# A hybrid encoder layer on one core: modulation sums on two other engines, and three weight blocks kept one quarter later

## The chip, the cores and the metric

The kernel runs on one core of a Trainium2 chip. The core has a matrix engine (TensorE, PE in the profile), three engines for elementwise work (VectorE as DVE, ScalarE as ACT, GpSimd as POOL), and SyncE (SP), whose queue issues nearly all DMAs here. Each engine executes its own instructions strictly in order and waits on semaphores for the others. The metric is the device time of one execution in microseconds, median of several runs.

## The reference, cut to what matters

One layer: a mixer and a SwiGLU feed-forward block over 2048 positions of 1024 channels, both modulated by six vectors that are computed from one conditioning vector `c`.

```python
c_act = silu(c)
mod = (c_act @ w_ada + b_ada)                  # w_ada is 1024 x 6144
sh1, sc1, g1, sh2, sc2, g2 = split(mod, 6)
h = x * (1.0 + sc1) + sh1
p = h @ w_in                                   # 1024 x 3328, 13 blocks of 256 columns
y = concat(conv_module(...), hgrn2_mixer(...), chunk_attention(...)) @ w_out
x = layer_norm(ALPHA * x + (1.0 + g1) * y)
h = x * (1.0 + sc2) + sh2
gt, up = split(h @ w_ffn_in, 2)
y = (silu(gt) * up) @ w_ffn_out
x = layer_norm(ALPHA * x + (1.0 + g2) * y)
```

## The kernel before

All arithmetic is float32. Each big matmul is done as three passes over operands that are split into a high and a low part: ScalarE casts the high part (`split`, L230), VectorE or GpSimd subtracts it for the low part (L231).

The mixer works through four quarters of 512 positions (`for q in range(NQ)`, L791). A quarter projects the modulated input with the 13 column blocks of `w_in`, runs 62 convolution taps on VectorE (L377), four recurrent heads (`rec_head`), the attention, and the output projection with four blocks of `w_out`. In `rec_head` GpSimd subtracts (L460, and six times L493, tile `tmp<-recB`), ScalarE takes exponentials, VectorE multiplies (L462, L496 to L503), and TensorE multiplies the results (`ktp`, `lp`). The feed-forward part follows from about 1230 us on.

The modulation vector is a sum over the 1024 rows of `w_ada`, each row scaled by an entry of `cact`. The kernel holds 128 rows at a time on the partitions, so a column stretch is a sum of eight scaled tiles (`acc += st * sc`); a matmul with ones then adds over the partitions (`mps`, `rps`).

- `start` (L274) does this for `sh1` and `sc1` (variable `part` 0 and 1) in four steps `kp` of 256 columns. A step loads 8 row tiles of 128x256 for each part (two per DMA, tile `ada_w`), sums them into `tmp`, gets `mod1`, modulates two tiles of the input (`ft`, L239), splits them (`hh`, `hl`), and multiplies them by a quarter of the rows of three weight blocks: the convolution's gate B_AG, its values B_AV, and the first head's B_REC (L308).
- `ada_rest` (L708) is a generator for the other four vectors: eight sums of eight 128x512 tiles (`xb`) into `adac` (L159, L161). The quarter loop advances it by one sum after a head (L810).

Weights: `load_w` (L247) loads a raw quarter block (256 KB), splits it, and stores the split pair (512 KB, `wki<-whl`, L245) to device memory. Later quarters load the stored pair instead of splitting again (`whl<-wki`). Split pairs wait in four buffers (tag `whl`), raw ones in three, the `xb` tiles in four that the output projection uses as well.

The order of each engine's instructions is set by a scheduler that places them by priority and by estimated times; `shifted(tc, -BOOST)` raises a priority. So an edit in one place can move instructions elsewhere.

Of the kernel before, what the change touches and what calls it, by code (L numbers as in the profile page):

```python
# [11 lines left out]
AF = mybir.ActivationFunctionType  # L12
ALU = mybir.AluOpType
# [95 lines left out]
def mixer_phase(tc, es, env):  # L109
    nc = tc.nc  # L110
    NQ = env["NQ"]
    x, xT, bias_d, w_ada, w_in, w_out, rows = (env[k] for k in ("x", "xT", "bias", "w_ada", "w_in", "w_out", "rows"))
    ident, ones, epsc, cact = (env[k] for k in ("ident", "ones", "epsc", "cact"))
# [21 lines left out]
    def tmp(w=Q):  # L135
        return pt.tile([P, 640], F32, name="tmp", tag="tmp", bufs=N_TMP)[:, 0:w]
# [7 lines left out]
    def psum(name):  # L144
        return pm.tile([P, Q], F32, name=name, tag="pm")
# [7 lines left out]
    nc.scalar.activation(out=e0, in_=e0, func=AF.Exp)  # L153
    nc.vector.tensor_tensor(out=cact, in0=c0, in1=e0, op=ALU.mult)

    def add_ada(st, acc, kt, c0):
        nc.sync.dma_start(out=st, in_=w_ada[kt * P:(kt + 1) * P, c0:c0 + 512])
        if kt == 0:
            nc.vector.tensor_scalar(out=acc, in0=st, scalar1=cact[:, 0:1], scalar2=None, op0=ALU.mult)  # L159
        else:  # L160
            nc.vector.scalar_tensor_tensor(out=acc, in0=st, scalar=cact[:, kt:kt + 1], in1=acc,  # L161
                                           op0=ALU.mult, op1=ALU.add)

    def load_ada(alloc, acc, c0):
        for kt in range(KT):
# [2 lines left out]
    def cols_out(acc, ps, dst, one, bc, n=4):  # L168
        for j in range(n):
            nc.tensor.matmul(out=ps[:, j:j + 1], lhsT=acc[:, j * P:(j + 1) * P], rhs=ones[:, 0:1],  # L170
                             start=True, stop=True)
        nc.vector.scalar_tensor_tensor(out=dst, in0=ps[:, 0:n], scalar=one, in1=col(bc, n),
                                       op0=ALU.add, op1=ALU.add)
# [45 lines left out]
    for a in atm:  # L219
# [4 lines left out]
    wkept = {k: tc.dram_tile([4, P, 2, 2, 256], F32R, name=f"wk{k[0]}{k[1]}")  # L224
             for k in [("i", b) for b in range(D_IN // 256)] + [("o", b) for b in range(4)]}
    kept = set()
    state, uhist, kvprev = {}, {}, {}

    def split(src, hi, lo, eng=nc.vector):
        nc.scalar.copy(out=hi, in_=src)  # L230
        eng.tensor_tensor(out=lo, in0=src, in1=hi.bitcast(F32), op=ALU.subtract)  # L231
# [12 lines left out]
    def move(dst, src):  # L244
        nc.sync.dma_start(out=dst.bitcast(F32), in_=src.bitcast(F32))  # L245

    def load_w(key, order, eng=None):  # L247
        parts = {}
        src = (w_in if key[0] == "i" else w_out)[key[1]]
        for kp in order:  # L250
            w = pa.tile([P, 2, 2, 256], F32R, name="whl", tag="whl", bufs=N_W)
            parts[kp] = hi, lo = w[:, 0], w[:, 1]
            if (key, kp) in kept:
                move(w, wkept[key][kp])
                continue
            raw = pa.tile([P, 2, 256], F32, name="wraw", tag="wraw", bufs=N_WRAW)
            nc.sync.dma_start(out=raw, in_=src[:, kp * 2:kp * 2 + 2, :])
            split(raw, hi, lo, eng or (nc.gpsimd if kp % 2 else nc.vector))
            move(wkept[key][kp], w)
            kept.add((key, kp))  # L260
        return parts

    def proj_f(b):
# [10 lines left out]
    def start():  # L274
        nst = 0
        ps = {b: [pool.tile([P, Q], F32, name="pjt", tag=tag) for _ in range(2)]
              for b, pool, tag in ((B_AG, pj, "pj"), (B_AV, pj, "pj"), (B_REC, pm, "pm"))}
        for kp in range(4):
            c0 = kp * 256
            for part in range(2):  # L280
                acc = tmp(256)
                for kk in range(4):
                    i = nst % 22
                    nst += 1
                    if i >= 14:
                        st = pt.tile([P, 2, 256], F32, name="ada_w", tag=f"attk{i % 4}", bufs=2)
                    else:
                        st = pa.tile([P, 2, 256], F32, name="ada_w", tag=f"y{'hl'[i % 2]}{1 + i // 2}")
                    r0 = kk * 256
                    nc.sync.dma_start(out=st, in_=w_ada[r0:r0 + 256, part * D + c0:part * D + c0 + 256].rearrange(  # L290
                        "(k p) c -> p k c", p=P))
                    for k in range(2):
                        sc = cact[:, 2 * kk + k:2 * kk + k + 1]
                        if kk == 0 and k == 0:
                            nc.vector.tensor_scalar(out=acc, in0=st[:, k], scalar1=sc, scalar2=None, op0=ALU.mult)
                        else:
                            nc.vector.scalar_tensor_tensor(out=acc, in0=st[:, k], scalar=sc, in1=acc,
                                                           op0=ALU.mult, op1=ALU.add)
                o = part * 8 + kp * 2
                cols_out(acc, psum("mps"), mod1[:, o:o + 2], float(part),  # L300
                         (C_BSC1 if part else C_BSH1) + kp * 2, 2)
            load_h(0, (2 * kp, 2 * kp + 1))
            for n, b in enumerate(ps):
                w = load_w(("i", b), (kp,), nc.gpsimd if n else nc.vector)[kp]
                for k in range(2):
                    for j in range(2):
                        for n, (a, c) in enumerate(PASSES):
                            nc.tensor.matmul(out=ps[b][j], lhsT=w[a][:, k, j * P:(j + 1) * P],  # L308
                                             rhs=hts[2 * kp + k][c], start=(kp == 0 and k == 0 and n == 0),
                                             stop=(kp == 3 and k == 1 and n == 2))  # L310
        return ps
# [479 lines left out]
    for q in range(NQ):  # L791
        us, k0, V, G = nxt
        if q == 2:
            h2_norm(tc, env, 0)
            h2_norm(tc, env, 1)
        taps = conv_taps(us)
        accs = None
        kbm = k0
        for h in range(4):
            rec_head(q, h, kbm, V, G[h % 2])  # L800
            for _ in range(TAPS[h] if h < 3 else 0):
                accs = next(taps, accs)
            if h == 2:
                conv_back(accs)
            if h < 3:
                kbm = rec_front(h + 1)
            if h == 1:
                V = rec_v(1)
                G = rec_g(1)
            if h < 3 or q == 0:  # L810
                next(rest, None)
            if q >= 2:
                for _ in range(2):
                    next(early, None)
        kvq = att_front(q)
        attention(q, kvq)
        if q + 1 == NQ:
            for _ in rest:
                pass
            as_.close()  # L820
            rs_.close()
            ffn_open(tc, env)
        else:
            nxt = fronts_a(q + 1)
        out_proj(q)
# [389 lines left out]
```

## Time and profile before

| | |
|---|---|
| median of 3 runs | 2593.28 us (2588.7, 2593.28, 2594.78) |
| the profiled execution | 2589.91 us, span of its instructions 2588.2 us |
| TensorE, matmuls | busy 2457.8 us, 95% of the span |
| VectorE | busy 1656.1 us, 64% |
| ScalarE | busy 997.2 us, 39% |
| GpSimd | busy 665.7 us, 26% |
| mean granted TensorE clock | 0.974 |
| DMA | 423.99 MB, mean 164 GB/s |

Busy TensorE time is not the same as full speed: matmuls are pipelined, and at a granted clock of 0.5 the same work takes twice as long. So the share is read stage by stage, and the idle time of TensorE with what ended it counts for more than its sum.

### The profile page before, as it was taken

What the parts mean: (1) busy time and instruction counts of PE and PEld (TensorE: products, weight loads), DVE (VectorE), ACT (ScalarE), POOL (GpSimd) and SP (SyncE); (2) the same over time, 40 slices, a digit from 0 to 9 for tenths busy, and PEclk for the clock granted to TensorE, in tenths of its full rate; (3) what the DMA queues carried; (4) which work ended last, traced back from release to release, by engine and by line L of the source; (5) the groups of instructions that cost most, each with busy time, mean ns of one, the idle gap of its engine ahead of it and who ended that gap; (6) DMA issues with size and microseconds to landing.
All of it is one profiled execution on the core that took longest, in us unless ns stands there. A gap on an engine that the chain in (4) does not pass through costs nothing.

```text
span 2588.2 us, 36360 instructions
## 1 busy us (share of the span) xinstructions
PE 2457.8 (95%) x13274; PEld 2078.5 (80%) x13274; DVE 1656.1 (64%) x2917; ACT 997.2 (39%) x1920; POOL 665.7 (26%) x571
## 2 busy tenths in 40 slices
PE   6888899999999999987999999999999999999998
PEld 5766799879977898876878788888888888888887
DVE  7987696669557785666655555765445474364666
ACT  2444444354244433544323333433333352242333
POOL 3433112200152112510333332332322211111121
PEclk8997999999999999988999999999999999999999
DMA  9676667663755645547333332442222274454544
GB/s 354 212 236 187 186 197 264 201 180 128 241 183 172 205 164 184 191 135 259 102 117 119 118 130 90 164 142 91 74 82 90 74 244 142 130 182 134 161 147 142
DMA packets 202691, 423.99 MB, mean 164 GB/s; under 512 B 20240, under 2 KB 69008, under 8 KB 202512
## 3 DMA queue, kind: packets, MB, share of 16 engines
q1 hardware_dynamic: 202352, 421.15, 49.8%
q8 instruction: 104, 1.70, 0.3%
q14 instruction: 75, 0.61, 0.1%
q0 software_dynamic: 160, 0.52, 0.1%
HBM read 317.78 MB, written 95.42 MB: 160 GB/s over the span
## 4 chain that ended last, share of the span: by engine, by line
PE 78%; DVE 10%; DMA 6%; issue 3%; ACT 2%; POOL 1%; SPq 0%; DVEq 0%; POOLq 0%; ACTq 0%
PE pi L953 31%; PE po L1095 17%; PE pjt L270 11%; PE pjt L321 9%; PE lp L513 2%; DVE cacc L377 2%; PE sc L625 1%; PE tp L661 1%; PE tp L648 1%; DMA whl<-wki 1%; DMA whl<-wko 1%; PE lp L533 1%; DMA xst<-zall 1%; DMA opraw<-srcd 1%; DMA xb<-in_x_dram 1%
## 5 line engine op out<-in xcount | busy, mean ns | idle before, releaser
L953 PE MATMUL pi<-oph,fhi 128*128 128x512 f32 x1232 | 484.1, 393 | 17.8 <-ACT fhi L829 11.9
L953 PE MATMUL pi<-opl,fhi 128*128 128x512 f32 x1232 | 483.7, 393 | 0.0
L953 PE MATMUL pi<-oph,flo 128*128 128x512 f32 x1232 | 478.9, 394 | 0.0
L270 PE MATMUL pjt<-hh,whl 128*128 128x512 f32 x1184 | 402.5, 411 | 16.2 <-DMA whl<-wki 6.4
L953 PEld LDWEIGHTS pi<-oph,fhi 128*128 128x128 f32 x1232 | 232.4, 189 | 70.2 <-ACT fhi L829 12.1
L829 ACT CAST fhi<-fraw 128x512 fp32r<-128x512 f32 x220 | 136.2, 621 | 392.3 <-PE pi L953 376.6
L270 PEld LDWEIGHTS pjt<-hh,whl 128*128 128x128 f32 x1184 | 227.4, 194 | 66.4 <-DMA whl<-wki 6.0
L958 DVE TENSOR_TENSOR fu<-fu,pi 128x512 f32<-128x512 f32 x176 | 120.8, 686 | 245.8 <-PE pi L953 245.1
L953 PEld LDWEIGHTS pi<-opl,fhi 128*128 128x128 f32 x1232 | 232.5, 189 | 52.3
L1095 PE MATMUL po<-oph,alo 128*128 128x512 f32 (+1 forms) x702 | 273.9, 390 | 0.0
L1095 PE MATMUL po<-oph,ahi 128*128 128x512 f32 (+1 forms) x702 | 270.1, 385 | 3.1 <-DVE res L1116 3.1
L1095 PE MATMUL po<-opl,ahi 128*128 128x512 f32 (+1 forms) x702 | 272.6, 388 | 0.0
L953 PEld LDWEIGHTS pi<-oph,flo 128*128 128x128 f32 x1232 | 232.3, 189 | 49.5 <-DVE flo L830 0.2
L830 DVE TENSOR_TENSOR alo<-araw,ahi 128x512 fp32r<-128x512 f32 x172 | 148.5, 871 | 190.9 <-ACT ahi L829 174.3
L270 PE MATMUL pjt<-hl,whl 128*128 128x512 f32 x592 | 243.0, 411 | 0.0
L321 PE MATMUL pjt<-whl,yh 128*128 128x256 f32 x1024 | 196.7, 288 | 15.5 <-DMA whl<-wko 12.0
L830 DVE TENSOR_TENSOR flo<-fraw,fhi 128x512 fp32r<-128x512 f32 x220 | 159.5, 742 | 70.9 <-ACT fhi L829 70.8
L377 DVE SCALAR_TENSOR_TENSOR cacc<-u,cs,cacc 128x512 f32<-128x512 f32 x240 | 195.3, 843 | 0.2
L829 ACT CAST ahi<-araw 128x512 fp32r<-128x512 f32 x172 | 104.9, 618 | 222.3 <-PE po L1095 208.0
L321 PEld LDWEIGHTS pjt<-whl,yh 128*128 128x128 f32 x1024 | 164.1, 194 | 17.7 <-DVE yl L231 7.9
L930 POOL TENSOR_TENSOR ft<-fraw 128x512 f32<-128x512 f32 x43 | 59.9, 1392 | 450.6 <-DMA fraw<-in_w_fi_dram 433.5
L1095 PEld LDWEIGHTS po<-oph,ahi 128*128 128x128 f32 x702 | 132.4, 189 | 31.7 <-DVE res L1116 3.3
(257 smaller groups left out, 4539.1 us busy)
## 6 DMA issues: line engine op xcount, KB each, us to landing
whl<-wki SPq DMA_DIRECT2D x156, 512.0 KB, 3.8
fraw<-in_w_fi_dram SPq DMA_DIRECT2D x86, 512.0 KB, 3.7
araw<-actd SPq DMA_DIRECT2D x154, 256.0 KB, 3.4
wki<-whl SPq DMA_DIRECT2D x52, 512.0 KB, 4.3
whl<-wko SPq DMA_DIRECT2D x48, 512.0 KB, 3.5
actd<-fs SPq DMA_DIRECT2D x44, 512.0 KB, 3.3
xb<-in_w_ada_dram SPq DMA_DIRECT2D x64, 256.0 KB, 4.7
opraw<-srcd SPq DMA_DIRECT2D x56, 256.0 KB, 5.0
```

What stands on the lines that cost most here:

```text
L270: nc.tensor.matmul(out=ps[j], lhsT=w[kt // 2][a][:, kt % 2, j * P:(j + 1) * P], rhs=hts[kt][c], start=(kt == 0 and n == 0), stop=(kt == KT ...
L321: nc.tensor.matmul(out=ps[tt // 2][:, tt % 2, :], lhsT=lhs[2 * kp + k][c][:, tt * P:(tt + 1) * P], rhs=w[kp][a][:, k, :], start=(ko == 0 a ...
L377: nc.vector.scalar_tensor_tensor(out=ac, in0=us[j][:, t:t + Q], scalar=col(wc + t), in1=ac, op0=ALU.mult, op1=ALU.add)
L513: nc.tensor.matmul(out=lp[0:n, c, :], lhsT=ddf[:, c * P:c * P + n], rhs=d4[:, c, :, :], start=True, stop=True)
L533: nc.tensor.matmul(out=lp[:, c, :], lhsT=K[:, 2 * i + c, :], rhs=M[:, 2 * i + c, :], start=True, stop=True)
L625: nc.tensor.matmul(out=sc[:, 0:n + x], lhsT=qs[hd][ph][:, i * P:(i + 1) * P], rhs=kt_[:, o - x0:o - x0 + n + x], start=ph == 0, stop=ph == 1)
L829: nc.scalar.copy(out=hi, in_=src)
L830: nc.vector.tensor_tensor(out=lo, in0=src, in1=hi.bitcast(F32), op=ALU.subtract)
L930: e.tensor_tensor(out=t1, in0=w12, in1=w11, op=ALU.subtract)
L953: nc.tensor.matmul(out=out, lhsT=w[n][a][:, idx, :], rhs=ops[n, idx][c], start=first and idx == 0 and i == 0, stop=idx == NK - 1 and i == ...
L958: nc.vector.tensor_tensor(out=out, in0=a, in1=b, op=ALU.add)
L1095: nc.tensor.matmul(out=pts[j][:, c], lhsT=a[x][:, j * P:(j + 1) * P], rhs=wo[f][y][:, c], start=f == 0 and m == 0, stop=f == NF - 1 and m ...
```

## The change

Three edits.

1. A helper `add_scaled` multiplies a tile by its scalar on ScalarE, in place (into the accumulator for the first tile), and adds it to the accumulator on GpSimd. It is used for the `sc1` half of the sums in `start` and for all sums of `ada_rest`; the `sh1` half stays on VectorE.
2. `start` no longer stores the split pairs of its three blocks (`keep=False`). The second quarter finds nothing kept, loads their raw tiles again, splits them and stores the pairs then; quarters three and four load the pairs as before.
3. `ada_rest` advances after heads 0 to 2 in the first quarter, after all four heads in the second, and after heads 1 and 3 in the third; before, after all four heads in the first quarter and after heads 0 to 2 in each later one.

```diff
+    def add_scaled(acc, st, sc, first):
+        nc.scalar.activation(out=acc if first else st, in_=st, func=AF.Copy, scale=sc)
+        if not first:
+            nc.gpsimd.tensor_tensor(out=acc, in0=acc, in1=st, op=ALU.add)
+
     def add_ada(st, acc, kt, c0):
         nc.sync.dma_start(out=st, in_=w_ada[kt * P:(kt + 1) * P, c0:c0 + 512])
-        if kt == 0:
-            nc.vector.tensor_scalar(out=acc, in0=st, scalar1=cact[:, 0:1], scalar2=None, op0=ALU.mult)
-        else:
-            nc.vector.scalar_tensor_tensor(out=acc, in0=st, scalar=cact[:, kt:kt + 1], in1=acc,
-                                           op0=ALU.mult, op1=ALU.add)
+        add_scaled(acc, st, cact[:, kt:kt + 1], kt == 0)
...
-    def load_w(key, order, eng=None):
+    def load_w(key, order, eng=None, keep=True):
...
-            move(wkept[key][kp], w)
-            kept.add((key, kp))
+            if keep:
+                move(wkept[key][kp], w)
+                kept.add((key, kp))
...
-                        if kk == 0 and k == 0:
+                        first = kk == 0 and k == 0
+                        if part:
+                            add_scaled(acc, st[:, k], sc, first)
+                        elif first:
...
-                w = load_w(("i", b), (kp,), nc.gpsimd if n else nc.vector)[kp]
+                w = load_w(("i", b), (kp,), nc.gpsimd if n else nc.vector, False)[kp]
...
-            if h < 3 or q == 0:
+            if q == 1 or q == 2 and h % 2 or q == 0 and h < 3:
                 next(rest, None)
```

The lines of the changed kernel stand one to five below those of before (L231 becomes L232, L493 becomes L498).

GpSimd's order in `start`, before: the splits of the weights (`whl`) and of the odd input tiles (`hl1`, `hl3`, `hl5`, `hl7`, two digits of the buffer number follow).

```order
L231 TENSOR_TENSOR whl_342<-wraw_343,whl_342 128x512
L231 TENSOR_TENSOR whl_360<-wraw_361,whl_360 128x512
L231 TENSOR_TENSOR hl1_320<-ft_317,hh1_319 128x512
L231 TENSOR_TENSOR hl3_430<-ft_427,hh3_429 128x512
L231 TENSOR_TENSOR whl_452<-wraw_453,whl_452 128x512
L231 TENSOR_TENSOR whl_470<-wraw_471,whl_470 128x512
L231 TENSOR_TENSOR hl5_540<-ft_537,hh5_539 128x512
```

The same place in the changed kernel, from the second weight split to `hl1`; `tmp_289`, `tmp_403` and `tmp_517` are the `sc1` sums of steps 0, 1 and 2 (of the 15 adds between, the last ten are shown).

```order
L159 TENSOR_TENSOR tmp_403<-tmp_403,ada_w_409 128x256
L159 TENSOR_TENSOR tmp_289<-tmp_289,ada_w_307 128x256
L159 TENSOR_TENSOR tmp_403<-tmp_403,ada_w_415 128x256
L159 TENSOR_TENSOR tmp_289<-tmp_289,ada_w_307 128x256
L159 TENSOR_TENSOR tmp_403<-tmp_403,ada_w_415 128x256
L159 TENSOR_TENSOR tmp_517<-tmp_517,ada_w_518 128x256
L159 TENSOR_TENSOR tmp_403<-tmp_403,ada_w_421 128x256
L159 TENSOR_TENSOR tmp_517<-tmp_517,ada_w_523 128x256
L159 TENSOR_TENSOR tmp_403<-tmp_403,ada_w_421 128x256
L159 TENSOR_TENSOR tmp_517<-tmp_517,ada_w_523 128x256
L232 TENSOR_TENSOR hl1_327<-ft_324,hh1_326 128x512
```

What followed the second weight split directly now stands behind 15 adds of three steps.

VectorE's order at the end of the first quarter, in the third head, before: `adac` are sums of `ada_rest`, L462 and L496 belong to the head.

```order
L161 SCALAR_TENSOR_TENSOR adac_2035<-xb_2039,cact_69,adac_2035 128x512
L464 COPY recel_1736<-tmp_1730 128x4
L466 TENSOR_TENSOR recqe_1738<-tmp_1730,recM_1480 128x512
L161 SCALAR_TENSOR_TENSOR adac_2035<-xb_2042,cact_69,adac_2035 128x512
L420 SCALAR_TENSOR_TENSOR ft_2015<-pjt_1961,ft_2014 128x512
L421 SCALAR_TENSOR_TENSOR ft_2016<-pjt_1961,ft_2014 128x512
L462 TENSOR_TENSOR tmp_1732<-tmp_1732,recK_1478 128x512
L555 SCALAR_TENSOR_TENSOR tmp_1368<-recG_949,tmp_1368 128x512
L161 SCALAR_TENSOR_TENSOR adac_2035<-xb_2045,cact_69,adac_2035 128x512
L556 SCALAR_TENSOR_TENSOR tmp_1367<-tmp_1367,tmp_1368 128x512
L161 SCALAR_TENSOR_TENSOR adac_2035<-xb_2048,cact_69,adac_2035 128x512
```

VectorE no longer has the sums between; they stand on GpSimd, around the same head's subtractions (L465 and L498, on L460 and L493 before), in the changed kernel:

```order
L159 TENSOR_TENSOR adac_1728<-adac_1728,xb_1752 128x512
L465 TENSOR_TENSOR tmp_1762<-recB_1502 128x512
L159 TENSOR_TENSOR adac_1728<-adac_1728,xb_1756 128x512
L232 TENSOR_TENSOR whl_2261<-wraw_2262,whl_2261 128x512
L612 MEMSET bias_t_2558 64x64
L613 MEMSET bias_t_2558 64x64
L159 TENSOR_TENSOR adac_2065<-adac_2065,xb_2069 128x512
L159 TENSOR_TENSOR adac_2065<-adac_2065,xb_2073 128x512
L498 TENSOR_TENSOR tmp_1788<-recB_1502 128x512
L498 TENSOR_TENSOR tmp_1800<-recB_1502 128x512
```

Of the second and third sum, nine adds stand ahead of the six subtractions and five behind them.

## Rows read from the trace of the kernel before

**Rows 1.** Windows: span, busy time and count by engine, clock, DMA.

```profile
core 0: us, PE busy (x) PEld busy (x) DVE busy (x) ACT busy (x) POOL busy (x), PEclk, DMA share, GB/s
0.00:250.00 250.00, 197.30 (x1048) 165.08 (x1048) 210.21 (x350) 100.78 (x201) 89.98 (x93) 0.89 0.75 249
250.00:600.00 350.00, 333.99 (x2138) 290.80 (x2139) 258.32 (x558) 160.01 (x355) 60.17 (x60) 0.98 0.64 203
1230.00:1900.00 670.00, 664.10 (x2917) 543.46 (x2917) 378.14 (x534) 230.07 (x387) 222.88 (x156) 1.00 0.33 113
```

**Rows 2.** Waits of TensorE, 0 to 250 us: total, times, longest.

```profile
PE lp L513 <- DVE tmp L501: 14.0, 3, 7.2
PE mps L170 <- DVE tmp L297: 13.7, 3, 11.4
PE ktp L469 <- DVE tmp L462: 8.5, 2, 6.3
```

**Rows 3.** Windows of the first 225 us, as in rows 1.

```profile
10.00:58.00 48.00, 36.69 (x135) 29.02 (x136) 44.35 (x88) 10.72 (x19) 14.02 (x11) 0.86 1.05 376
...
65.00:171.00 106.00, 90.94 (x548) 77.65 (x547) 104.72 (x151) 51.86 (x106) 44.27 (x30) 0.95 0.63 200
...
187.00:205.00 18.00, 4.43 (x15) 2.69 (x14) 14.67 (x17) 11.85 (x26) 10.52 (x10) 0.62 0.84 311
205.00:225.00 20.00, 17.32 (x88) 15.61 (x89) 18.49 (x40) 3.08 (x8) 0.00 (x0) 0.57 0.41 132
```

**Rows 4.** VectorE groups by line, 0 to 65 us: busy, mean ns, idle before.

```profile
L297 DVE SCALAR_TENSOR_TENSOR tmp<-ada_w,cact,tmp 128x256 f32<-128x256 f32 x56 | 28.7, 538 | 1.5 <-DMA ada_w<-in_w_ada_dram 0.7
...
L295 DVE TENSOR_SCALAR tmp<-ada_w,cact 128x256 f32<-128x256 f32 x8 | 3.3, 417 | 1.0 <-DMA ada_w<-in_w_ada_dram 1.0
```

**Rows 5.** Timeline of VectorE: start, duration, instruction.

```profile
32.17 4.87 DVE L297 SCALAR_TENSOR_TENSOR tmp<-ada_w,cact,tmp 128x256 f32<-128x256 f32 x6
...
37.23 2.96 DVE L297 SCALAR_TENSOR_TENSOR tmp<-ada_w,cact,tmp 128x256 f32<-128x256 f32 x6
...
88.36 7.69 DVE L377 SCALAR_TENSOR_TENSOR cacc<-u,cs,cacc 128x512 f32<-128x512 f32 x5
```

**Rows 6.** Timeline of GpSimd.

```profile
14.04 2.79 POOL L231 TENSOR_TENSOR whl<-wraw,whl 128x512 fp32r<-128x512 f32 x2 [3.88 <-ACT whl L230]
...
31.94 2.74 POOL L231 TENSOR_TENSOR whl<-wraw,whl 128x512 fp32r<-128x512 f32 x2
...
53.68 1.28 POOL L231 TENSOR_TENSOR hl<-ft,hh 128x512 fp32r<-128x512 f32 x1
...
89.54 8.85 POOL L493 TENSOR_TENSOR tmp<-recB 128x512 f32<-128x512 f32 x6
...
195.33 7.93 POOL L493 TENSOR_TENSOR tmp<-recB 128x512 f32<-128x512 f32 x6
203.22 1.06 POOL L526 TENSOR_TENSOR tmp<-recB 128x256 f32<-128x256 f32 x1
```

**Rows 7.** Timeline of TensorE; brackets: idle time before, and what ended it.

```profile
16.41 2.92 PE L308 MATMUL pjt<-hh,whl 128*128 128x512 f32 x6 [1.64 <-ACT hh L230]
...
194.53 1.09 PE L469 MATMUL ktp<-ident,tmp 128*128 128x128 f32 x4 [6.26 <-DVE tmp L462]
...
205.64 1.09 PE L513 MATMUL lp<-tmp 128*64 128x64 f32 x8 [7.23 <-DVE tmp L501]
```

**Rows 8.** Timeline of ScalarE.

```profile
61.44 1.28 ACT L334 ACTIVATE ft<-pjt 128x512 f32<-128x512 f32 x2 [3.08 <-PE pjt L308]
...
199.99 0.40 ACT L494 ACTIVATE tmp<-tmp 128x256 f32<-128x256 f32 x1
```

**Rows 9.** Windows of line 161 alone, the sums of `ada_rest`.

```profile
165.00:225.00 60.00, 18.34 (x21) 0.74 0.72 244
...
330.00:480.00 150.00, 9.61 (x12) 1.00 0.67 221
```

**Rows 10.** Chain that ended last: start, duration, what.

```profile
289.93 7.22 DMA whl<-wki
```

## The prediction

> **What bounds the kernel now.** I read windows of the whole span first [rows 1]. From 1230 us on TensorE is busy 664.1 of 670 us, and the edits leave that part alone. From 250 to 600 us it idles 16 of 350 us. In the first 250 us it idles 52.7 us, at a clock of 0.89: what the change is worth is decided there. Next the waits of TensorE in that stretch [rows 2]: all three long ones end on VectorE, on sums of `start` (L297, 13.7 us) and on the multiplies of a recurrent head (L501 14.0, L462 8.5). Then shorter windows [rows 3]: from 10 to 58 us VectorE is busy 44.35 of 48 us and the DMA engines are full (share 1.05, 376 GB/s); from 65 to 171 us VectorE is busy 104.72 of 106 us, with the taps, and sets the pace; from 187 to 205 us TensorE works 4.43 of 18 us, and its clock reads 0.57 until 225.
>
> **The start, 0 to 65 us.** VectorE loses 28 sums of 538 ns and 4 of 417 ns [rows 4], 16.7 us, and seven or eight sums of the first `ada_rest` group. ScalarE gets 32 multiplies at 0.40 us [rows 8], 12.8 us, beside 10.72 us of work in 48 [rows 3]: hidden. GpSimd gets 28 adds of 128x256. None stands in the trace before. Bounds: half of a 128x512 subtraction, 7.93/6 = 1.32 us, so 0.66; and the strided 128x256 subtraction, 1.06 us [rows 6]. I take 0.72, half of the splits (2.79/2 and 2.74/2) and a little.
>
> GpSimd's order then gives the time. Its second weight split ends at 14.04 + 2.79 = 16.8 us [rows 6]. From there to `hl7`, the last input split, stand 26 small adds, 7 large ones and 10 splits: 26 x 0.72 + 17 x 1.37 = 42 us, so 58.8 us. It also stands idle once, before `hl1`: that needs `ft`, and on VectorE `ft` stands behind 17 sums and splits of later steps. Beside GpSimd's two-input work VectorE gets about one instruction done for each of GpSimd's (6 sums take 4.87 us beside two splits, 2.96 us alone; 5 taps take 7.69 us beside the subtractions [rows 5]), so `ft` comes at about 29 us and `hl1` some 3 us after the adds. `hl7` then ends near 62 us, against 53.68 + 1.28 = 55.0 [rows 6]. TensorE's first projection matmul moves from 16.4 us [rows 7] to about 30. That costs less than it looks: before, TensorE worked off its backlog until the gate's activations at 61.44 us [rows 8]; now the gate is complete four matmuls after `hl7`, at about 63.5, and one more us goes for a clock that may be low. Term: +3 us; bounds -3 (0.66 per add, no idle) and +12 (1.06 per add: 26 x 0.34 = 8.8 more).
>
> The 12 stores of 512 KB that leave the start (6.3 MB, 16.7 us at 376 GB/s) earn nearly nothing there: in rows 4 the sums waited 0.7 + 1.0 us for DMAs in all, so the full DMA engines were not what came last. The taps from 65 to 171 us carry the +3 along: VectorE has the same work there.
>
> The Trainium skill (SBUF — State Buffer, section "SBUF: two separate sides") says that GpSimd and a VectorE instruction with two SBUF inputs take one shared pair of ports in turn, each for its whole instruction. Rows 5 agree: 1.54 us a tap beside the subtractions. By that rule a GpSimd add costs VectorE about as long as the sum it saved, where both are busy; it is the fourth case below.
>
> **The end of the first quarter, 171 to 225 us.** Before, 21 sums of L161 run here on VectorE, 18.34 us of it [rows 9], and in its order they stand ahead of the head's L462 and between it and L496. They wait for `xb` tiles, and the head waits with them: TensorE idles 6.26 us before `ktp` and 7.23 us before the first `lp` [rows 7], 13.6 of 18 us in all, and then runs slowly [rows 3]. After, VectorE holds none of them, and one group of eight is gone to the second quarter. The sums' tiles still come through the same queue, so the wait doesn't vanish: ScalarE's exponential now stands behind five multiplies that wait for tiles, and GpSimd's six subtractions stand behind nine adds. But the fifth and later tiles of the group at the subtractions no longer hold anything of the head. I put `ktp` 5 us earlier, the first `lp` 6 us, and the last, paced by subtractions of 1.32 us instead of VectorE's crowded queue, 8 us; with 2 us for matmuls that now run at 0.57 clock. Term: -10 us; bounds 0 (the wait only moves to ScalarE and GpSimd) and -16 (all 13.6 us of idle time and the 2.7 after it).
>
> **The second quarter.** Twelve loads of 512 KB become twelve of 256 KB, a cast (0.64 us [rows 8]) and a subtraction (1.37 us on GpSimd for six, some 0.7 us on VectorE for the other six), and twelve stores of 512 KB. ScalarE gets 7.7 us, GpSimd 8.2, VectorE 4.2, the DMA engines 3.1 MB more, 8 us at the rate of the start, over some 100 us in a stretch where they are 0.64 busy [rows 1]. The chain that ended last passes through one such load once, 7.22 us [rows 10]: a half-size load should land sooner, the split eats that. Stored buffers come free later. Term: +1 us; bounds -3 and +5. The cover is TensorE's own backlog, 334 of 350 us; where it is gone, one load with its split, some 5 us, shows.
>
> **The later sums.** In quarters two and three VectorE loses some 28 sums (12 cost 9.61 us [rows 9]) and GpSimd gains 35 adds at 1.37 us, 48 us, over 400 us in which it is hardly used (60 of 350 us [rows 1]). TensorE's idle time there is too small for a gain. What is queued behind an add is a head's subtractions, and attention and the output projection fill TensorE meanwhile. Term 0; bounds -3 and +4.
>
> **Sum.** +3 - 10 + 1 + 0 = -6 us. The profiled execution took 2589.91 us, 1.7 over its span; it lies 3.4 under the median and 1.8 under the mean of the four executions known, 2591.7. So -6 gives 2584 against it and 2586 against the mean; I take 2586.
>
> **Rivals.**
> - *The head gains everything, the start nothing is lost* (2574): the adds cost 0.66 us, VectorE's freed 16.7 us bring `ft` early, and both idle stretches go: -2 - 15 = -17. For it: VectorE is the engine that every long wait names. Against it: GpSimd's long order in the start.
> - *The wait changes its engine* (2592): `xb` tiles come no sooner, ScalarE's multiplies hold the exponentials as long as VectorE's sums held the multiplies. The end of the quarter gains 3, the start loses 3. For it: four `xb` buffers before and after, and a round trip for each. Against it: a group fewer in the stretch.
> - *GpSimd and VectorE hold each other up* (slower, 2603): in the start 15 adds stand beside VectorE's remaining sums; if each also pays the 0.41 us of one sum, `hl7` comes 6 us later, +9. From 171 to 225 us each of 14 large adds keeps one VectorE instruction out for 1.54 - 0.74 = 0.8 us, 11 us, which turns -10 into +1. With +1 for the weights: +11. It decides as soon as the adds near the head find VectorE busy more than half of the time. For it: rows 5. Against it: VectorE has gaps there once the sums are off it.
>
> **How the numbers follow.** The forecast has 0.47, and 2580 to 2592 as its own range; of the rivals the full gain has 0.19, the moved wait 0.15, the slower one 0.19. A measurement of this kernel can tell about 0.2%, 5.2 us, so faster means under 2588.1 against the median. That is 0.34 of the forecast's 0.47 and all of the first rival: 0.53. Within: 0.13 and the second rival, 0.28. Slower: the last, 0.19. The terms' bounds added up would reach from -22 to +21; they hardly all come at once, and 8 in 10 I expect between 2574 and 2602.
>
> **What would show it.** In the profile after: small adds near 0.72 us on GpSimd; the first L313 matmul near 30 us; the gate's first activation at 63 to 65 us (earlier than 61: the start was judged too dear; after 70: the third rival). VectorE still full until about 174 us. The idle time of TensorE between 187 and 215 us less by half, and `ktp` not behind `adac` any more. From 250 us on, the same distance to the end as before within 4 us. The forecast is wrong if TensorE waits as long for ScalarE's or GpSimd's part of that head, or if windows from 250 to 600 us show new waits for `whl`.

## The result, and the profile after

The changed kernel takes 2636.76 us (median of 4 runs, 2632.41 to 2641.85). The kernel before takes 2593.64 us (median of 4, 2588.70 to 2594.78). The ratio is 1.0179, 95% interval 1.0162 to 1.0197; these two medians divided give 1.0166, inside that interval. The forecast was 2586 us with a range up to 2602: it is 51 us too fast, and the sign is wrong.

The windows of the changed kernel, with the columns of [rows 1]:

```profile
10.00:58.00 48.00, 27.64 (x114) 22.61 (x113) 32.57 (x44) 26.03 (x53) 39.97 (x42) 1.00 0.86 280
...
0.00:250.00 250.00, 186.25 (x990) 158.32 (x991) 182.39 (x273) 119.92 (x243) 141.61 (x139) 0.90 0.66 213
250.00:600.00 350.00, 317.75 (x1960) 274.62 (x1960) 248.41 (x476) 173.81 (x370) 109.83 (x95) 0.93 0.62 201
1274.00:1944.00 670.00, 664.01 (x2916) 543.78 (x2915) 378.99 (x535) 229.87 (x387) 221.70 (x156) 0.99 0.33 113
```

The last line is the feed-forward stretch, read 44 us later than in [rows 1]: TensorE is busy 664.01 us against 664.1 before. The whole loss stands ahead of it. VectorE was relieved as meant: 182.39 us busy in the first 250 us instead of 210.21 [rows 1], 32.57 instead of 44.35 of the 48 us from 10 to 58 us [rows 3]. TensorE lost 11.05 us of busy time in the first 250 us all the same, and 16.24 us from 250 to 600 us, where the forecast saw nothing. In that second stretch its granted clock fell as well, from 0.98 to 0.93, so more work went than the busy time says.

What TensorE waits for in the first 250 us (total, times, longest, as in [rows 2]):

```profile
PE mps L171 <- POOL tmp L159: 16.1, 1, 16.1
PE lp L518 <- DVE tmp L506: 9.7, 2, 5.0
PE mps L171 <- DVE tmp L302: 9.3, 1, 9.3
PE pjt L313 <- ACT hh L231: 6.5, 2, 3.4
PE lp L515 <- DVE tmp L508: 4.9, 3, 2.0
PE rps L179 <- POOL adac L159: 4.5, 1, 4.5
```

Two of the six name GpSimd's adds, and none of the three in [rows 2] does. The wait for ScalarE's casts (`hh`) is not new: it was the fourth longest before, 5.6 us.

To see where time goes between kernels I use one derived number. TensorE's busy time multiplied by the granted clock, summed over windows of 5 us, says how much work it has done; the *lag* is how much later a kernel reaches the sum that the kernel before has at 475 us (the second quarter's third head) and at 600 and 900 us (inside the attention of the second and of the third quarter). It is good for steps within one kernel. At 900 us it differs from the measured difference of the whole run by up to some 16 us, so what is said of a kernel's time goes by the measured ratios. The first tap of the convolution (67.52 us before) needs no such sum; the expectations below read the tap behind it, about 1 us later (68.6 and 84.9 us).

```text
                                     first tap   lag at 475  600  900   ratio to before (95%)
after                                    83.87        11   38   45   1.0179 (1.0162-1.0197)
e1  start sums alone                     71.34         4    7   10   0.9980 (0.9962-0.9999)
e2  later sums alone                     69.47        -8    1    0   1.0009 (0.9993-1.0026)
e3  weights alone                        72.61        -1    0    8   0.9970 (0.9956-0.9984)
e4  places alone                         67.77       -13   -5    5   0.9993 (0.9971-1.0015)
e5  both sums                            78.48         8   14   13   1.0070 (1.0046-1.0093)
e6  later sums, places                   67.94         0   21   28   1.0128 (1.0102-1.0154)
e7  all but later sums                   77.49        -9    1   13   1.0054 (1.0035-1.0072)
e8  all but places                       83.20        13   21   20   1.0057 (1.0036-1.0077)
e9  after, first group on VectorE        77.22        -1   25   31   1.0102 (1.0080-1.0124)
e10 after, three places a quarter        83.13        13   24   40   1.0137 (1.0118-1.0156)
e11 after, loads issued by GpSimd        82.19        17   54   71   1.0262 (1.0242-1.0282)
e12 before, weights, three places        73.60       -16  -15   -5   0.9986 (0.9969-1.0004)
e13 after, later adds on VectorE         79.43        -2    9   23   1.0067 (1.0042-1.0092)
e14 after, later multiplies on VectorE   85.19         3   26   32   1.0157 (1.0126-1.0187)
e15 after, head's subtractions moved     83.30        15   40   45   1.0154 (1.0124-1.0184)
e16 before, weights, last groups late    73.50       -17  -15  -13   0.9966 (0.9953-0.9979)
e17 after, no memsets                    83.53        16   44   53   1.0188 (1.0151-1.0226)
e18 e15 and e17                          83.36        13   37   44   1.0152 (1.0123-1.0181)
```

So in the changed kernel 11 us are lost by 475 us, 27 more by 600 us and 7 more by 900 us. Of the 27, 24 come between 475 and 525 us.

### The profile page after: what moved, and what is told of

Read it like the earlier page. It is cut to its first block, busy times and chain, and to the rows that moved or that the text cites. A ratio compares the mean times of both kernels' runs of the same rounds, so it can differ in the third digit from the quotient of the medians.

```text
span 2632.5 us, 36545 instructions
## 1 busy us (share of the span) xinstructions
PE 2467.8 (94%) x13274; PEld 2085.7 (79%) x13274; DVE 1638.2 (62%) x2827; ACT 1053.6 (40%) x2028; POOL 774.1 (29%) x661
## 4 chain that ended last, share of the span: by engine, by line
PE 74%; DVE 12%; DMA 8%; ACT 2%; issue 2%; POOL 1%; SPq 1%; DVEq 0%; ACTq 0%; POOLq 0%
PE pi L958 31%; PE po L1100 17%; PE pjt L272 9%; PE pjt L326 8%; DVE cacc L382 4%; PE lp L518 3%; PE sc L630 1%; PE tp L666 1%; DMA xb<-in_w_ada_dram 1%; DMA ada_w<-in_w_ada_dram 1%; PE tp L653 1%; DMA whl<-wki 1%; PE lp L538 1%; POOL adac L159 1%; DVE tmp L501 1%
## 5 line engine op out<-in xcount | busy, mean ns | idle before, releaser
L1051 POOL TENSOR_TENSOR res<-res,row 128x512 f32<-128x512 f32 x32 | 50.6, 1587 | 384.1 <-ACT res L1050 381.7
```

The source lines that it names most:

```text
L1051: nc.gpsimd.tensor_tensor(out=r, in0=r, in1=ga, op=ALU.mult)
```

## The parts alone: e1 to e4

Each of these is the kernel before with one part of the change.

e1: `if part: add_scaled(...)` in `start` only.

> Only the sc1 half of the start's sums goes to ScalarE multiplies and GpSimd adds; all else as before. Theory A (the serial chain of multiplies and adds on two in-order engines costs the time): the first tap stands near 80 us instead of 68.6, and about 12 us of it are kept to the end: some 2605 us. Rival B (the twelve raw reloads in the second quarter, and the places of the later groups, cost the time): the start is made good by the first quarter's attention, 2593 to 2598 us.

e2: `add_scaled` in `add_ada` only.

> Only the later modulation sums go to ScalarE and GpSimd; places as before, so three or four groups fall in the first quarter. Theory A: 2610 to 2625 us, since every group puts multiplies that wait for their tiles in front of the heads' exponentials, and adds in front of the heads' subtractions. Rival B: 2590 us, since the VectorE work of 18 us at the end of the first quarter goes.

e3: `keep=False` in `start` only.

> Only the first three weight blocks are left unstored in the first quarter, loaded raw, split and stored in the second. Theory A: within 4 us of before, 2590 to 2597 us. Rival B: 2605 to 2618 us, with the wait of 542 to 571 us on SyncE's queue (whl behind xb) in the second quarter.

e4: only the new condition of `next(rest)`.

> Only the places of the later groups move: one group fewer in the first quarter, one more after the second quarter's last head, fewer in the third. Theory A: within 4 us of before, or up to 6 us faster at the end of the first quarter. Rival B: 2600 to 2610 us, since the group after the last head of the second quarter stands in SyncE's queue ahead of the loads of the next quarter.

No part alone makes the kernel slower: e1 and e3 are a little faster, e2 and e4 the same. Theory A missed on e1 and e2, rival B on e3 and e4. On e1 and e3 the other theory was a little off too: both kernels came out faster than its range. The four ratios add up to 0.5% faster, and the whole is 1.8% slower. The cost is in how the parts meet.

## Parts together: e5 to e8

e5 is e1 and e2 together; e6 is e2 and e4; e7 and e8 are the whole change without `add_scaled` in `add_ada` and without the new condition.

> The start's sums and the later sums together on ScalarE and GpSimd, with the places and the stores of before. Theory A (the two sums collide in the start: the first later group's multiplies, which wait for xb tiles, stand on ScalarE ahead of the casts of the last input tiles, and its adds stand between the start's adds on GpSimd): first tap at 80 us or later, 2603 to 2610 us. Rival C (only all parts together cost): first tap near 72 us, 2590 us.

> The later sums on ScalarE and GpSimd at the new places, the start as before. Theory A (a group after the second quarter's last head is harmless on VectorE, but on ScalarE and GpSimd it stands in front of that head's and the next quarter's work): the second quarter's attention starts 20 us later after its last head than before, third quarter up to 10 us more, 2615 to 2625 us. Rival C: no loss in the second quarter, 2588 to 2594 us.

> All of the change but the later sums, which stay on VectorE. Theory A: the start costs 3 us, nothing is lost later: 2585 to 2594 us. Rival B (stores and places cost once the start is later): 2610 us or more, with the loss at the end of the second quarter.

> All of the change but the new places of the later groups. Theory A: the loss of the start stays, the 23 us at the end of the second quarter go: 2600 to 2610 us. Rival B (the raw reloads of the weights cost the second quarter): 2625 us or more.

e6 and e8 came out as theory A expected, and e5 nearly: its time lies in the range, its first tap a little under the 80 us. e7 did not: 1.0054 where it allowed no loss, and its lag shows why: 9 us ahead at 475 us, it loses 10 by 600 and 12 more by 900 us, as e4 loses 8 and 10 with the same places. Two meetings cost most. The later sums and the new places, harmless alone, cost 1.28% (33 us) together, and the lag shows 21 us of it between 475 and 600 us. The two kinds of sums cost 0.70% (18 us) together: 11.0 us are there at the first tap, and by the lag 8 at 475 us and 14 at 600.

**The start.** The first tap comes 3.8 us later with the start's sums alone (e1), 5.1 with the weights alone (e3), 10.0 with these two and the places (e7), 11.0 with both sums (e5), 15.7 with sums and weights (e8) and 16.4 after. So the start's sums cost about 4 us, the weight edit 5 to 6, and the first later group, which falls into the start, about 7 beside the start's sums (alone, in e2, 2.0). e9 tests that last piece: in the changed kernel the first group's sum goes back to VectorE.

```diff
-        add_scaled(acc, st, cact[:, kt:kt + 1], kt == 0)
+        if c0 != 2 * D:
+            add_scaled(acc, st, cact[:, kt:kt + 1], kt == 0)
+        # else: the two VectorE instructions of before
```

> The changed kernel, with only the first later group (the one that falls into the start) back on VectorE. Theory A (that group's multiplies and adds stand in the start's path on ScalarE and GpSimd): first tap near 77 us instead of 84.9, the end 7 us earlier, 2628 to 2631 us. Rival D (the start is late from its own small adds and the changed order of loads alone): first tap within 2 us of 84.9, 2635 us or more.

The first tap came at 77.22 us, as theory A said, and the end about 20 us earlier, not 7: the ratio fell from 1.0179 to 1.0102, and the lag at 475 us from 11 to -1, so some of it was won after the start. e13 and e14 below tell which half of that group's work it is: with the later adds on VectorE the first tap comes at 79.43 us, with the later multiplies on VectorE at 85.19. So some 4.4 of the 6.7 us go with the adds on GpSimd, and taking the multiplies alone off ScalarE wins nothing here. GpSimd has the group's seven large adds between the small ones, and the last `sc1` sum ends behind them; VectorE then needs its column sum (`mod`) for the last input tiles. From the changed kernel (start, duration, instruction; in brackets the idle time before and what ended it):

```profile
62.80 0.73 POOL L159 TENSOR_TENSOR tmp<-tmp,ada_w 128x256 f32<-128x256 f32 x1
```

```profile
64.70 0.16 DVE L173 SCALAR_TENSOR_TENSOR mod<-mps,cs 128x2 f32<-128x2 f32 x1 [8.65 <-PE mps L171]
```

ScalarE adds some more:

```profile
60.11 0.73 ACT L157 ACTIVATE xb<-xb,cact 128x512 f32<-128x512 f32 x1 [5.14 <-DMA xb<-in_w_ada_dram]
...
65.96 0.72 ACT L157 ACTIVATE xb<-xb,cact 128x512 f32<-128x512 f32 x1 [1.76 <-DMA xb<-in_w_ada_dram]
66.59 0.60 ACT L231 CAST whl<-wraw 128x512 fp32r<-128x512 f32 x1
67.09 1.14 ACT L231 CAST hh<-ft 128x512 fp32r<-128x512 f32 x2
75.62 0.60 ACT L339 ACTIVATE ft<-pjt 128x512 f32<-128x512 f32 x1 [7.39 <-PE pjt L313]
```

Two multiplies of `ada_rest` wait for their tiles, and the casts of a weight block and of the last two input tiles stand behind them. TensorE's last step of projections then starts at 67.76 us and the gate's activation at 75.62, against 61.44 [rows 8]. In e9 the last cast of `hh` stands at 62.95 us, in e1 at 60.54. The weight edit's 5 us are bound to the queue: in e3 the last load of an input tile is issued at 50.81 us instead of 44.10, behind four loads of `xb`. That it is this load alone which holds the start was not tried.

The prices of the new instructions, from the same trace (nanoseconds: minimum, median, maximum):

```profile
L159 POOL TENSOR_TENSOR adac<-adac,xb x56: 1259/1293/1788, 40.5 to 804.0; 128x512 f32<-128x512 f32 x56
L159 POOL TENSOR_TENSOR tmp<-tmp,ada_w x28: 724/902/1192, 9.4 to 62.8; 128x256 f32<-128x256 f32 x28
```

A small add takes 0.90 us, not the 0.72 of the forecast; the least is 0.72.

## Which engine: e10, e11, e13 and e14

e10 asks whether it is the group behind the second quarter's last head. The changed kernel has `if h < 3` instead of its condition.

> The changed kernel with three places in each quarter (after heads 0, 1, 2), none after the last head. Theory A (the group behind the second quarter's last head is what delays attention and the next quarter's front, and the late groups of the third quarter cost 10 us more): the idle time from 500 to 600 us falls by 15 to 20 us, 2606 to 2615 us. Rival D (three groups in the second quarter cost as much as four): 2630 us or more.

It came between the two: 1.0137. The lag grows by 11 us instead of 27 between 475 and 600 us, as theory A said, and by 16 more in the third quarter, where the group now stands. So the stretch behind the last head is dear, but a group moved out of it is dear where it goes.

e11 asks whether SyncE's queue, blocked by `xb` loads, is what holds the second quarter: `nc.gpsimd.dma_start` for `c0 >= 3 * D`.

> The changed kernel with the loads of the third and later groups issued from GpSimd instead of SyncE, so that no other transfer stands behind them. Theory E (SyncE's queue, blocked by xb loads from 514 to 536 us, is what holds the weights, the xT loads and the attention moves): 15 us or more of the second quarter's loss go, 2612 to 2622 us. Theory F (the in-order multiplies and adds on ScalarE and GpSimd hold the head themselves): 2632 to 2645 us.

It is slower still, 1.0262. TensorE now stands 22 us in one piece:

```profile
546.56 1.11 PE L474 MATMUL ktp<-ident,tmp 128*128 128x128 f32 x4 [22.28 <-DVE tmp L467]
```

and on GpSimd the head's subtraction L465, for which that multiply waits, stands behind loads and adds until 532.84 us:

```profile
517.97 0.14 POOL L612 MEMSET bias_t<- 64x64 f32 x1 [3.71 <-DMA bias_t<-in_bias_dram]
...
521.81 1.78 POOL L159 TENSOR_TENSOR adac<-adac,xb 128x512 f32<-128x512 f32 x1 [1.09 <-ACT adac L157]
...
532.26 0.55 POOL L162 DMA_DIRECT2D xb<-in_w_ada_dram  x1
532.84 1.05 POOL L465 TENSOR_TENSOR tmp<-recB 128x512 f32<-128x512 f32 x1
```

That shows what GpSimd's order can do to a head. It does not clear SyncE's queue, since the run filled another in-order engine instead.

e13 and e14 take the later sums off one engine each. e13: `nc.scalar.activation(...)`, then `nc.vector.tensor_tensor(... op=ALU.add)`. e14: `nc.vector.tensor_scalar(... op0=ALU.mult)`, then `nc.gpsimd.tensor_tensor(... op=ALU.add)`.

> The changed kernel, with the later sums as ScalarE multiplies and VectorE adds: ScalarE has the same work as in the changed kernel, GpSimd has none of these sums. Theory P (GpSimd's adds, in its order and on the ports it shares with VectorE, cost the time): most of the loss that the later sums bring goes, 2600 to 2612 us. Theory S (the multiplies on ScalarE, which wait for their tiles ahead of the heads' exponentials and casts, cost it): 2625 us or more.

> The changed kernel, with the later sums as VectorE multiplies and GpSimd adds: GpSimd has the same work, ScalarE none of it. Theory P: 2625 us or more. Theory S: 2600 to 2612 us.

This settles the engine. With ScalarE's multiplies kept and the adds off GpSimd, 1.0067: about as much as the kernel without these sums on other engines (e7, 1.0054). With the multiplies off ScalarE and the adds kept on GpSimd, 1.0157, close to the whole change. What the later sums cost is the GpSimd half of them; theory P held.

GpSimd in the changed kernel where the second quarter ends:

```profile
484.69 4.69 POOL L159 TENSOR_TENSOR adac<-adac,xb 128x512 f32<-128x512 f32 x3 [19.07 <-ACT adac L157]
489.34 3.56 POOL L498 TENSOR_TENSOR tmp<-recB 128x512 f32<-128x512 f32 x3
492.86 1.72 POOL L159 TENSOR_TENSOR adac<-adac,xb 128x512 f32<-128x512 f32 x1
494.54 3.64 POOL L498 TENSOR_TENSOR tmp<-recB 128x512 f32<-128x512 f32 x3
...
515.70 0.14 POOL L612 MEMSET bias_t<- 64x64 f32 x1 [12.34 <-DMA bias_t<-in_bias_dram]
...
516.13 6.64 POOL L159 TENSOR_TENSOR adac<-adac,xb 128x512 f32<-128x512 f32 x5
523.11 2.63 POOL L159 TENSOR_TENSOR adac<-adac,xb 128x512 f32<-128x512 f32 x2 [0.35 <-ACT xb L157]
532.41 2.99 POOL L159 TENSOR_TENSOR adac<-adac,xb 128x512 f32<-128x512 f32 x2 [6.67 <-ACT adac L157]
535.36 1.22 POOL L465 TENSOR_TENSOR tmp<-recB 128x512 f32<-128x512 f32 x1
...
542.11 3.00 POOL L159 TENSOR_TENSOR adac<-adac,xb 128x512 f32<-128x512 f32 x2 [0.39 <-ACT xb L157]
545.08 8.58 POOL L498 TENSOR_TENSOR tmp<-recB 128x512 f32<-128x512 f32 x6
```

Three groups pass here, from 484.69 to 545.11 us: 60.4 us. In e13 the same three groups take 42.9 us on VectorE, from 466.93 to 509.82:

```profile
466.93 2.91 DVE L165 TENSOR_TENSOR adac<-adac,xb 128x512 f32<-128x512 f32 x3 [0.59 <-ACT adac L163]
...
506.38 0.69 DVE L165 TENSOR_TENSOR adac<-adac,xb 128x512 f32<-128x512 f32 x1 [1.21 <-ACT xb L163]
508.33 1.49 DVE L165 TENSOR_TENSOR adac<-adac,xb 128x512 f32<-128x512 f32 x2 [1.26 <-ACT xb L163]
```

They share one accumulator (`adac` has one buffer), so a group's first multiply waits until TensorE has read the sum of the group before (`ACT adac L157` ends GpSimd's idle time twice in these rows and three times in the whole trace, 42.8 us), and four `xb` tiles, so each load waits for an add. Behind these loads stands everything else that SyncE issues. In the changed kernel:

```profile
514.58 21.18 SPq L162 DMA_DIRECT2D xb<-in_w_ada_dram  x11
535.85 0.38 SPq L246 DMA_DIRECT2D whl<-wki  x1
...
542.23 10.75 SPq L246 DMA_DIRECT2D whl<-wki  x3
```

and in e13, where eight weight loads go out from 507.57 us on:

```profile
502.91 1.88 SPq L162 DMA_DIRECT2D xb<-in_w_ada_dram  x2
...
507.57 27.61 SPq L248 DMA_DIRECT2D whl<-wki  x8
```

How long SyncE's `xb` loads wait for these sums from 484 to 545 us (total, times, longest), in the changed kernel and then in e13:

```profile
SPq L162 <- POOL adac L159: 18.9, 14, 3.1
SPq L162 <- ACT adac L157: 10.3, 3, 6.1
```

```profile
SPq L162 <- ACT adac L163: 5.5, 1, 5.5
...
SPq L162 <- DVE adac L165: 2.3, 3, 1.5
```

That is 29.2 us against 7.8. In the changed kernel no weight load is issued from 495.42 to 535.85 us, 40.4 us; in e13 the same gap is 23.6 us (478.87 to 502.49).

TensorE works 92.44 of the 116 us from 484 to 600 us in the changed kernel, and 106.78 in e13:

```profile
484.00:600.00 116.00, 92.44 (x494) 77.20 (x493) 74.36 (x119) 56.45 (x111) 48.05 (x42) 0.87 0.56 176
```

```profile
484.00:600.00 116.00, 106.78 (x580) 90.69 (x581) 84.83 (x194) 61.90 (x127) 10.31 (x16) 0.93 0.56 181
```

TensorE does not stand waiting for the late weights. From 250 to 600 us that wait is short:

```profile
PE pjt L272 <- DMA whl<-wki: 0.7, 3, 0.3
```

What changed is the order of its instructions, which the scheduler sets when the kernel is built. Take the stretch from the state update of the second quarter's third head (its last `up`) to the end of the convolution's variance (the last `var`). There the kernel before has 108 matmuls of projections between the head's own, and the changed kernel has none. So every short wait of that head shows, and the clock falls with it. The changed kernel from there, and the kernel before at the same place:

```profile
494.00:528.00 34.00, 22.23 (x114) 17.41 (x113) 22.95 (x38) 20.02 (x39) 18.32 (x19) 0.75 0.50 166
```

```profile
481.00:514.00 33.00, 32.18 (x213) 27.23 (x211) 23.79 (x51) 14.61 (x31) 2.35 (x6) 1.00 0.74 248
```

TensorE is busy for 3.94 of the 10 us from 494 us, and in the 10 us behind them the granted clock is 0.56, so most of them ran at the lower of its two levels. The count of these filling matmuls goes with the loss between 475 and 600 us in all the kernels of the table. Ten besides the kernel before have 57 to 131 of them (e13 75, e7 65) and lose 1 to 11 us there by the lag. Nine have 0 to 19 and lose 21 us or more, except e4 (19 of them, 8 us). No run holds TensorE's order fixed, so whether the late tiles themselves or only the order that was made for them costs the time is not shown.

VectorE's own work there slows down beside the adds. The head's convolution end has two instructions (L411, in e13 L413) that take 3.46 us in the changed kernel and 1.28 us in e13:

```profile
542.20 3.46 DVE L411 SCALAR_TENSOR_TENSOR tmp<-cacc,tmp 128x512 f32<-128x512 f32 x2
```

```profile
528.48 1.28 DVE L413 SCALAR_TENSOR_TENSOR tmp<-cacc,tmp 128x512 f32<-128x512 f32 x2
```

The Trainium skill (SBUF — State Buffer, section "Who interferes with whom") says that a VectorE instruction with two SBUF inputs contends with a GpSimd instruction that reads SBUF. By that rule L411 pays for each add beside it, and the rows agree: 1.73 us for one in the changed kernel, 0.64 in e13. It is not peculiar to the adds: in e13 the same instruction takes 1.52 to 1.59 us in the third and fourth quarter, where GpSimd does a head's subtractions. The Trainium skill (GPSIMD Engine Reference, section "4.1 Engine selection") also puts an elementwise add on VectorE, and GpSimd at about twice as slow with two inputs; the trace agrees: here a 128x512 add takes 1293 ns on GpSimd in the median and 0.69 us on VectorE (e13, 506.38 us).

## What in GpSimd's order: e15, e17 and e18

e15 moves the last head's subtractions of the second quarter to VectorE: `sub = nc.vector if q == 1 and h == 3 else nc.gpsimd`, used in L465, L498 and L531. e17 leaves out the two memsets L612 and L613, before which GpSimd stands 12.34 us, and so two masked corners of the attention; e18 does both.

> The changed kernel, with the eight subtractions of the second quarter's last head on VectorE instead of GpSimd, where they stand behind fourteen adds. If the order on GpSimd is what holds that head: 10 to 15 us won, 2620 to 2627 us. If VectorE's own slower instructions beside the adds hold it, or the transfers: within 4 us of 2636 us.

> The changed kernel without the two 64x64 memsets on each bias tile, so its attention lacks these two masked corners. In the changed kernel GpSimd stands idle 12.34 us before such a memset, until 515.70 us, with eight adds behind it. If that wait is what lets the adds and so the xb tiles come late: 10 to 15 us won, 2621 to 2627 us. If the adds are late for their own tiles: within 4 us of the changed kernel's ratio of 1.018.

> As the run before, and the eight subtractions of the second quarter's last head on VectorE as well; the two masked corners are left out here too. If both what stands ahead of the adds and what stands behind them hold the head: 15 to 22 us won, 2614 to 2622 us. If neither does and the loss is in the pace of the adds and VectorE's slower instructions beside them: no more than the 6 us of moving the subtractions alone, 2628 us or more.

e17 gained nothing (1.0188). The wait stayed and only changed its name:

```profile
516.73 1.26 POOL L159 TENSOR_TENSOR adac<-adac,xb 128x512 f32<-128x512 f32 x1 [11.87 <-ACT adac L157]
```

So the memset was not what came last. The next group's first multiply was, and that waits for TensorE's reading of the accumulator, which TensorE reaches in its own order at 514.87 us here and at 512.79 us in the changed kernel. e15 and e18 came to 1.0154 and 1.0152; their intervals overlap that of the changed kernel, and between 475 and 600 us e15 lags as much (25 us against 27). Moving what stands behind the adds is worth some 6 to 9 us by the ratios, if anything; the first of the two answers that e15 was to tell apart is not borne out, the second only in part. What is left, by exclusion, is the slow passage of the groups: with it SyncE's queue, the order that the scheduler gives TensorE around it, and VectorE's slower instructions beside it. How these share the loss was not separated.

## The third quarter, and a faster version: e12 and e16

`ada_rest` has eight groups in all, so the two advances of the changed kernel in the third quarter, and the three before, run one group: at 703 to 716 us before, at 789 to 804 us after. In the changed kernel and every other one with that later place (e4, e6, e7, e9, e11, e13 to e15, e17, e18) or with two groups in the third quarter (e10, e12) the lag grows by 5 to 17 us between 600 and 900 us, with the sums on either engine. With the places of before it does not in e2, e5 and e8; e1 (3 us) and e3 (8 us) are in between. In the changed kernel TensorE waits there for a row sum and then for the buffer behind it:

```profile
PE rps L179 <- POOL adac L159: 6.6, 1, 6.6
PE pjt L272 <- DVE xb L180: 3.8, 1, 3.8
```

and in e7, where VectorE adds:

```profile
PE rps L183 <- DVE adac L166: 3.8, 1, 3.8
PE pjt L276 <- DVE xb L184: 3.8, 1, 3.8
```

e12 is the kernel before with the weight edit and `if h < 3`; e16 has `if q < 2 and h < 3 or q == 2 and h < 1 or q == 3 and h < 2`, so that the third quarter gets no group more than before.

> The kernel before with the three weight blocks left unstored in the first quarter and three places per quarter; all sums stay on VectorE. Theory A: 10 us are won at the end of the first quarter and 6 in the weights, nothing is lost in the second quarter since no group stands behind its last head: 2575 to 2583 us. Rival D: the group that moves costs later what it gave: 2586 to 2592 us.

> The kernel before with the three weight blocks left unstored in the first quarter, three later groups in the first quarter, three in the second, one in the third and the last in the fourth; all sums on VectorE. Theory A: the 14 to 15 us that the two-edit version had won by 800 us stay, since the third quarter has fewer groups, not more: 2573 to 2580 us. Rival: the group costs the fourth quarter what it cost the third, 2583 to 2588 us.

e12 is within 0.2% of before, between the ranges of theory A and rival D: 16 us won by 475 us, 11 given back by 900 us. e16 keeps them: 0.9966 (0.9953 to 0.9979), 2578.11 us against 2587.03 for the kernel before on the same chip. It is faster than both kernels. Its ratio is the same as that of e3 alone (0.9970), so how much of it the places give beside the weights is not settled.

## Why the prediction was wrong, point by point

- **The later sums, "Term 0; bounds -3 and +4".** This is the step that failed. With the change's places these sums are worth about 30 us: 1.0179 against 1.0054 without them on other engines (e7) and 1.0067 with the adds on VectorE (e13). By the lag, 13 (against e13) to 20 us (against e7) of this are there by 475 us, where the first group counts most (e9: 12), and 16 to 17 come between 475 and 600 us, the stretch that the term speaks of. The step counted GpSimd's free time, 60 of 350 us busy, and let "attention and the output projection fill TensorE meanwhile". The runs show in its place: SyncE's `xb` loads wait 29.2 us for the adds and the accumulator (7.8 in e13), the weights of the next projections are issued up to 40 us apart behind them, and TensorE's order has no filling matmul left where it had 108. Which of these costs the time stays open; that it comes with the adds on GpSimd is shown by e13 and e14.
- **The start, "+3".** Measured 16.4 us at the first tap. As the cost of the start's sums alone the term was right (e1: 3.8). Two things were missed: the first later group, whose "7 large ones" were counted on GpSimd but cost about 7 us (e9, most of it with the adds), and the weight edit, taken to earn "nearly nothing" there, which costs 5 to 6. The small adds, 0.90 us instead of 0.72, are 26 x 0.18 = 4.7 us of GpSimd's order, and `hl7` ends at 69.72 us, not near 62. The first matmul of the projection came at 30.75 us (30 forecast), but the gate was not "complete four matmuls after `hl7`": all 36 matmuls of the last step begin at 67.76 us or later.
- **The end of the first quarter, "-10".** In the changed kernel this term came out about right. The same lag, read at more points, is 18 us at 170 us, 9 at 250 and 11 at 475: 7 to 9 us are won back. The wait before `ktp` there is 1.1 us, against 6.3 before. It is the places that give it and not VectorE's relief: in the same stretch, 170 to 250 us, e4 gains 12 us and e2 3; the 8 us that e2 is ahead at 475 us come after 250. With both edits (e6) 9 us are won by 250 us, and 5 of them are lost again by 475. The second rival, the wait that changes its engine, was right only in that a row sum now waits for GpSimd's adds (`rps`, 4.5 us, above).
- **The second quarter's weights, "+1".** By the lag of e3 nothing moves between 475 and 600 us (-1 and 0), as the term says. The whole run of e3 is 0.3% faster, 8 us, which lies outside the bounds of -3 and +5, on the good side. Why it gains was not studied.
- **The sum.** The terms' lower bounds add up to -25, not -22. That changes nothing in the range that was given.
- **The rivals.** "GpSimd and VectorE hold each other up" had the right sign and the right pair of engines, with 2603 us and a chance of 0.19. It looked at the start and at 171 to 225 us, and not at 484 to 600 us, where 27 of the 45 us of lag come.
- **What would show it.** "Windows from 250 to 600 us" was the right place to look: TensorE's busy time there fell from 333.99 to 317.75 us. The sign named, new waits for `whl`, is not there (0.7 us in all): TensorE's waits are short and name many lines, since what it lacks is work to fill with.

## What to carry to other kernels

An engine's share of idle time does not tell whether it can take a chain of work that shares a small pool of tiles and one accumulator: the chain's pace then sets when the tiles come free, and every transfer behind their loads in the same queue moves with it. Look too at the order of the engine that bounds the kernel: an edit elsewhere can take out the work that filled its waits. When edits that are harmless alone meet on the same in-order engines, price them together, at the places where their instructions stand in a row. And when such a meeting costs, take the work off one engine at a time, as e13 and e14 do, before explaining it from waits: one that looked like the cause (12.34 us before a memset) turned out not to matter.

## What the runs showed that was not expected

- Dependent adds of 128x256 on GpSimd spread from 724 to 1192 ns while VectorE was at work too, with 902 ns in the middle.
- A run of `xb` loads on SyncE took 21.18 us for 11 transfers, because each waited for a tile or for the accumulator (9 waits for adds, 10.7 us; 2 for a first multiply, 7.7 us). The same sums at the places of before cost nothing measurable (e2, 1.0009).
- Loads issued by GpSimd cost it 0.55 us each in its own order (e11, 532.26 us).
